# A hybrid attention layer on one core: the first output products placed among the last attention heads, operands in the tokens' tiles, and the end of mixer B left to the planner

## The chip, the core and the metric

The kernel runs on one core of one Trainium2 chip. The metric is device time in microseconds (us) for one execution. The core has a matrix engine (TensorE, "PE" in the profile, with its weight loads listed apart as "PEld"), three engines for elementwise work (VectorE "DVE", ScalarE "ACT", GpSimd "POOL") and a queue engine (SyncE "SP") that issues most of the DMA transfers. Each engine runs its own instructions in the order in which the program has them, and waits for the others by semaphores.

## The reference

One layer over 528 tokens (16 meta tokens and 512 real ones) of width 2048:

```python
hn = rmsnorm(h, pre_norm_g[layer])
proj = jnp.einsum('bld,dc->blc', hn, w_in[layer])
qa, ka, va, ga, qb, kb, vb, gb = jnp.split(proj, SPLIT_POINTS, axis=-1)
ya = gqa_axial_mixer(qa, ka, va, ...) * jax.nn.silu(ga)      # mixer A: 8 heads, 2 groups of keys
yb = diff_attn_mixer(qb, kb, vb, ...) * jax.nn.silu(gb)      # mixer B: 8 heads, differential, ALiBi
y = jnp.einsum('blc,cd->bld', jnp.concatenate([ya, yb], axis=-1), w_out[layer])
h = h + rmsnorm(y, post_norm_g[layer])
return h[:, N_META:, :]
```

Each mixer has heads of width 128. Only the 512 real tokens leave the layer.

## The kernel before

**Arithmetic.** Every large product is made from split operands: `x` is kept as a high part `xh` and a rest `xl`, a weight chunk as `wh` and `wl`, and a product is three matmuls (high by high, rest by high, high by rest). A weight chunk is 128 partitions by 1024 numbers (512 KB). SP loads it into `st`, ACT rounds it to `wh` (L156), DVE subtracts for `wl` (L157). `st`, `wh` and `wl` have three buffers each (pool `wp`, L115), and `fetch` (L199) keeps two chunks ahead of the one in use; the list `todo` sets their order.

**Stages.** First come the columns of mixer B, head by head: `dense_T` (L205) makes transposed columns by 16 steps `k` over the tokens' tiles `xh[k]`, `xl[k]`. Then mixer A's keys and values, the queries of both groups (`queries_A`, L678: four PSUM banks, 192 matmuls of 512 columns), the second group's keys and values, and eight gates (`dense_T(REAL)` in the loop at L841, 48 matmuls of 512 columns each). Last comes the output product.

**The planner.** The heads' work is written as generators (`attention_B`, `attention_A`, `p_times_v`, `finish_B`), and `Lanes` (L41) places it between the dense matmuls. It keeps a planned clock, which each matmul advances. `poll` (L81), called after each group of three dense matmuls, resumes a generator that is due; a generator says by `yield LAG[...]` how much later it is due again. `finish` (L96) and `finish_all` (L100) force: they resume generators one after the other until a head is done, with no dense matmul in between. PE keeps this order exactly. The planned clock is no measurement; it only sets the order. Transposes, `pv` and `ss` share two PSUM buffers (`tr`, pool `ptr`), so each of them also waits until ACT and DVE have read the one before the last.

**The two forced places.** After mixer A's first keys and values, L818 (`finish_head(NH - 1)`) forces the rest of mixer B's last head, since the queries of group 0 take over buffers of that head (`ql`) and the zeros `zed` (L819) take over those of `dist`. After the last gate, `gate_A(7, ...)` (L842, L555) and L845 force the rest of mixer A's last head. Then the attention's pools and the tokens' tiles are released (L846, L847), and the pools of the output product are opened in their place.

**The output product.** It is made as a Strassen-like scheme: 14 products of four weight chunks each (`product`, L936), a product being 48 matmuls of 512 columns into two PSUM banks (`po`). The columns of the output are taken in two pairs of blocks, `PAIRS` (L721). For a pair, `first_half` (L989) makes the product of operand `b0` (mixer B's heads, first half of the tokens), that of `t1` (difference of their halves), copies both to `y`, and adds the product of `of_a(0)` to the first bank pair and of `of_a(1)` to the second; `of_a` reads mixer A's gated heads `oh`/`ol`. Then come `t2`, `t3` and `t4`, sums of halves of both mixers. Some weight chunks are sums of blocks, made in DRAM beforehand (`ws`, `weigh`, L737). The gated heads reach these operands through DRAM (`oscr`): SP writes a head out (L543, L560) and reads it back in the layout that the product needs (L890, L901, L907), and ACT and DVE split it. `gpB` (1024 KB, the post-norm gains, L922) and the residual `xr` (L965) are loaded in this stage too. At the end of it rows are normalised and added to the residual (L1034 to L1081).

Of the kernel before, what the change touches and what calls it, by code (L numbers as in the profile page):

```python
# [17 lines left out]
P = 128  # L18
DM = 2048
# [86 lines left out]
def kernel(ctx: ExitStack, tc: tile.TileContext, xT, xn, xm, w_s, w_t, w_q, w_o,  # L106
# [571 lines left out]
    def queries_A(g):  # L678

        pss = [pd.tile([P, 512], F32, name="pd", tag="pd") for _ in range(TT)]  # L680
        for k0 in range(0, KT, 2):
# [64 lines left out]

    def wlast(i):
# [109 lines left out]
    b0, t1 = [[[op.tile([P, 2, NP], F32R, name=f"{n}{x}{i}", tag=f"{n}{x}{i}") for x in "hl"]
               for i in range(4)] for n in "ab"]
    oh, ol = [[op.tile([P, SEQ], F32R, name=f"o{x}{j}", tag=f"o{x}{j}") for j in range(NH)]
              for x in "hl"]  # L860
    t4 = [[op.tile([P, 2, NP], F32R, name=f"t4h{i}", tag=f"t4h{i}"),
           yp.tile([P, 2, NP], F32R, name=f"t4l{i}", tag=f"t4l{i}")] for i in range(4)]
    pad(op, "opad", 224)
    t3 = operand("t3", (yp, yp), 0, 1)
    yp.tile([P, 512], F32, name="jko", tag="jko")
    pad(yp, "ypad", 384)


    y = [[None] * 4 for _ in range(TT)]

    def fill(places):
        for t, g in places:
            y[t][g] = ytile(t, g)

    fill([(t, 3) for t in range(TT)])
    gpB = yp.tile([P, DM], F32, name="gpB")
    fill([(t, g) for t in range(3) for g in (1, 2)])
    fill([(t, 0) for t in range(TT)])
    pad(yp, "zpad", 128)
    t3 += operand("t3", (yp, yp), 1)  # L880
    t2 = operand("t2", (yp, yp))
    fill([(3, 1), (3, 2)])
    ssy = [yp.tile([P, 4], F32, name=f"ssy{t}", tag=f"ssy{t}") for t in range(TT)]
    sspart = [yp.tile([P, 1], F32, name=f"ssp{t}", tag=f"ssp{t}") for t in range(TT)]

    of_B = []
    for i in range(4):
        for g, half in ((3, lo_), (0, hi_)):
            st = y[i][g].rearrange("p (i q) -> p i q", i=2)
            nc.sync.dma_start(out=st, in_=oscr[i].rearrange("i p q -> p i q")[:, :, half])  # L890
            of_B.append(st)
    for i in range(4):
        st, sd = of_B[2 * i:2 * i + 2]
        split(b0[i], st)
        TTv(out=sd, in0=st, in1=sd, op=SUB)
        split(t1[i], sd)

    def bring_A(j):

        st = y[j // 2][1 + j % 2]  # L900
        nc.sync.dma_start(out=st, in_=oscr[4 + j // 2][j % 2])  # L901
        hi(oh[j], st)
        lo(ol[j], st, oh[j])

    def half_of(i, half):
        t = gp.tile([P, 2, NP], F32, name="ts", tag="g", bufs=4)
        load(t, oscr[i].rearrange("i p q -> p i q")[:, :, half])  # L907
        return t

    def sums_of_heads():  # L910
        for i in range(4):

            b1, r, c0, a0 = [half_of(n, half) for n, half in ((i, hi_), (4 + i, hi_), (i, lo_),
                                                              (4 + i, lo_))]
            for to, x, y_, op_ in ((t3, b1, r, SUB), (t2, r, c0, SUB), (t4, r, a0, ADD)):
                TTv(out=r, in0=x, in1=y_, op=op_)
                split(to[i], r)
                yield

    sum_steps = sums_of_heads()  # L920

    nc.sync.dma_start(out=gpB, in_=gpost)  # L922

    def square(t, g, src):
        jk = yp.tile([P, 512], F32, name="jko", tag="jko")
        at = (0, 1, 3, 2)[g]
        return nc.scalar.activation(jk, src, AF.Square, accum_out=ssy[t][:, at:at + 1])

    def by_gain(t, g, src=None):
        return TTv(out=y[t][g], in0=y[t][g] if src is None else src,  # L930
                   in1=gpB[:, g * 512:(g + 1) * 512], op=ALU.mult)
# [57 lines left out]
    def first_half(p, pool, tasks):  # L989


        r0, r1 = PAIRS[p]
        pa = product(of_t(b0), banks(pool), beside=tasks[0])
        rank[0] = 40
        for u, ps in enumerate(pa):
            nc.scalar.activation(y[u][r1], ps, AF.Copy)
        pb = product(of_t(t1), banks(pool), beside=tasks[1])
# [21 lines left out]
    for j in range(4):  # L1019
        bring_A(j)  # L1020
# [122 lines left out]
```

## Time and profile before

| | us |
|---|---|
| median of three runs (944.68 to 946.38) | 945.44 |
| the profiled execution | 945.67 |
| its span, first to last instruction | 943.9 |
| PE busy | 911.0 |
| DVE busy | 589.4 |
| ACT busy | 505.1 |
| POOL busy | 121.5 |

Matmuls overlap each other in PE's pipeline, so a row's duration is longer than the distance to the next row: a dense 512-column matmul has rows of 0.39 us that start 0.23 us apart. What a matmul costs is that distance. An idle stretch of PE stands in brackets behind the row that ends it, with the instruction that released it. "PEclk" is the clock that PE was granted as a share of full speed.

### The profile page before, as it was taken

The page shows a single profiled execution, that of the slowest core. Times are in us where ns is not written, and L with a number is a line of the kernel's source. Part 1 is how long each engine was busy: PE and PEld are TensorE (multiplying, and loading weights), DVE is VectorE, ACT ScalarE, POOL GpSimd, SP SyncE. Part 2 cuts the span into 40 slices and gives each one's busy share as a digit, 9 for nine tenths or more (in the row PEclk, how much of TensorE's full clock was granted, in tenths as well). Part 3 has the DMA queues.
Part 4 walks back from the last instruction along what each step waited for, and adds up shares of the span by engine and source line. Part 5 has one row for each costly group of instructions (what it writes and reads, how often), then busy time and mean ns, then how long its engine had stood idle before and what let it go on. Part 6 is the DMA issues. An engine that isn't in the chain of part 4 may idle for free.

```text
span 943.9 us, 14282 instructions
## 1 busy us (share of the span) xinstructions
PE 911.0 (97%) x5450; PEld 804.2 (85%) x5450; DVE 589.4 (62%) x1041; ACT 505.1 (54%) x877; POOL 121.5 (13%) x168
## 2 busy tenths in 40 slices
PE   9999999999999999999969999899999988999995
PEld 7999898989989899998958888888788876888884
DVE  6576675747575574856652464965454457766887
ACT  6564655647464563746632536556555546655552
POOL 0102120111112011110100201421111100000012
PEclk9999999999999999999979999999999999999998
DMA  9837645856848476682213322121212248879764
GB/s 327 288 112 222 158 136 136 235 130 181 210 118 241 122 199 170 172 219 68 80 45 101 89 91 68 45 67 57 79 57 90 79 135 307 280 257 329 262 214 178
DMA packets 52979, 149.86 MB, mean 159 GB/s; under 512 B 7920, under 2 KB 14960, under 8 KB 52528
## 3 DMA queue, kind: packets, MB, share of 16 engines
q1 hardware_dynamic: 48160, 132.18, 42.0%
q0 software_dynamic: 4608, 16.78, 10.3%
q8 instruction: 42, 0.69, 0.3%
q14 instruction: 25, 0.20, 0.1%
q10 hardware_dynamic: 144, 0.01, 0.0%
HBM read 140.55 MB, written 41.94 MB: 193 GB/s over the span
## 4 chain that ended last, share of the span: by engine, by line
PE 86%; DVE 5%; ACT 4%; DMA 3%; issue 1%; POOL 1%; SPq 0%; DVEq 0%; ACTq 0%; POOLq 0%
PE pd L60 57%; PE po L60 13%; PE sc L60 6%; PE pv L60 5%; PE tr L63 4%; DVE wl L157 1%; DVE y L1041 1%; DMA gpB<-in_gpost_dram 1%; ACT wh L156 1%; DMA st<-ws 1%; DMA xs<-in_xT_dram 1%; DMA st<-in_w_o_dram 0%; POOL ssh L245 0%; ACT jk L616 0%; PE ss L60 0%
## 5 line engine op out<-in xcount | busy, mean ns | idle before, releaser
L60 PE MATMUL pd<-xh,wh 128*128 128x264 f32 (+1 forms) x992 | 333.8, 337 | 0.2 <-ACT xh L184 0.2
L60 PE MATMUL pd<-xl,wh 128*128 128x264 f32 (+1 forms) x992 | 323.4, 326 | 0.4 <-DVE xl L185 0.4
L60 PE MATMUL pd<-xh,wl 128*128 128x264 f32 (+1 forms) x992 | 323.1, 326 | 0.1
L156 ACT ACTIVATE wh<-st 128x1024 fp32r<-128x1024 f32 (+2 forms) x159 | 165.7, 1042 | 231.1 <-PE pd L60 98.9
L157 DVE TENSOR_TENSOR wl<-st,wh 128x1024 fp32r<-128x1024 f32 (+2 forms) x159 | 191.3, 1203 | 118.5 <-ACT wh L156 117.3
L60 PEld LDWEIGHTS pd<-xh,wl 128*128 128x128 f32 x992 | 186.6, 188 | 16.3 <-DVE wl L157 0.3
L60 PEld LDWEIGHTS pd<-xh,wh 128*128 128x128 f32 x992 | 187.1, 189 | 11.7 <-ACT xh L184 0.7
L60 PEld LDWEIGHTS pd<-xl,wh 128*128 128x128 f32 x992 | 187.5, 189 | 10.1 <-DVE xl L185 0.8
L505 ACT ACTIVATE p<-p,mx 128x528 f32<-128x528 f32 x64 | 47.0, 734 | 43.2 <-DVE mx L497 43.0
L63 PE MATMUL tr<-ident,p 128*128 128x128 f32 (+1 forms) x320 | 50.9, 274 | 4.3 <-DVE qlA L333 3.2
L497 DVE CUSTOM_DVE_ANT_0 p<-sc,dist 128x528 f32<-128x528 f32 x64 | 44.8, 701 | 11.4 <-PE sc L60 11.0
L333 DVE TENSOR_TENSOR pl<-tr,ph 128x512 fp32r<-128x512 f32 x64 | 43.1, 686 | 13.1 <-ACT ph L330 12.4
L60 PE MATMUL pd<-wh,xh 128*128 128x512 f32 x128 | 51.2, 400 | 0.0
L60 PE MATMUL pd<-wh,xl 128*128 128x512 f32 x128 | 50.6, 396 | 0.0
L60 PE MATMUL pd<-wl,xh 128*128 128x512 f32 x128 | 50.5, 394 | 0.0
L330 ACT ACTIVATE ph<-tr 128x512 fp32r<-128x512 f32 x64 | 37.5, 592 | 23.5 <-PE tr L63 23.2
L63 PEld LDWEIGHTS tr<-ident,p 128*128 128x128 f32 (+1 forms) x320 | 37.1, 132 | 14.4 <-DVE qlA L333 3.8
L512 DVE SCALAR_TENSOR_TENSOR p<-p,c 128x528 f32<-128x528 f32 x32 | 24.5, 766 | 31.0 <-POOL p L510 31.0
L741 POOL DMA_DIRECT2D ws<-in_w_o_dram x32 | 26.7, 835 | 120.1 <-DMA ws<-in_w_o_dram 66.1
L599 POOL TENSOR_SCALAR p<-p,smA 128x528 f32<-128x528 f32 x32 | 23.4, 733 | 145.2 <-DVE smA L598 129.0
L510 POOL TENSOR_SCALAR p<-p,sm 128x528 f32<-128x528 f32 x32 | 23.5, 735 | 138.4 <-DVE sm L507 127.4
L457 POOL TENSOR_SCALAR pm<-pm 32x256 fp32r<-32x256 f32 x32 | 21.2, 662 | 143.7 <-ACT pm L330 140.9
(222 smaller groups left out, 1605.5 us busy)
## 6 DMA issues: line engine op xcount, KB each, us to landing
st<-in_w_t_dram SPq DMA_DIRECT2D x82, 512.0 KB, 4.2
ws<-in_w_o_dram POOLq DMA_DIRECT2D x32, 512.0 KB, 8.4
st<-ws SPq DMA_DIRECT2D x32, 512.0 KB, 4.9
st<-in_w_o_dram SPq DMA_DIRECT2D x24, 512.0 KB, 3.9
ws<-in_w_o_dram SPq DMA_DIRECT2D x16, 512.0 KB, 6.1
ws<-ws SPq DMA_DIRECT2D x16, 512.0 KB, 5.4
st<-in_w_q_dram SPq DMA_DIRECT2D x16, 512.0 KB, 3.5
xs<-in_xT_dram SPq DMA_DIRECT2D x16, 264.0 KB, 5.5
```

Of the source, the lines that this page charges most:

```text
L60: self._add(self.nc.tensor.matmul(out, lhsT, rhs, start=start, stop=stop, **kw), us)
L63: self._add(self.nc.tensor.transpose(out, in_, ident), 0.109)
L156: splits.append((nc.scalar.activation(wh[:, c], st[:, c], AF.Copy), nc.vector.tensor_tensor(out=wl[:, c], in0=st[:, c], in1=wh[:, c].bitca ...
L157: nc.vector.tensor_tensor(out=wl[:, c], in0=st[:, c], in1=wh[:, c].bitcast(F32), op=ALU.subtract)))
L330: nc.scalar.activation(dst, src, AF.Copy)
L333: nc.vector.tensor_tensor(out=dst, in0=src, in1=h.bitcast(F32), op=ALU.subtract)
L497: nc.vector.tensor_tensor_reduce(out=two(p), in0=sc[:, :, :HALF], in1=two(dist[:, w0:w0 + NT]), scale=-0.125 / slope(h), scalar=3.0e38, op ...
L505: nc.scalar.activation(p2[m], p2[m], AF.Exp, scale=-1.0, bias=mx[:, m:m + 1], accum_out=sm[:, m:m + 1])
L510: nc.gpsimd.tensor_scalar(out=p2[0], in0=p2[0], scalar1=sm[:, 0:1], scalar2=1.0, op0=ALU.mult, op1=ALU.mult)
L512: nc.vector.scalar_tensor_tensor(out=p2[0], in0=p2[1], scalar=c2, in1=p2[0], op0=ALU.mult, op1=ALU.add)
L599: nc.gpsimd.tensor_scalar(out=p, in0=p, scalar1=sm, scalar2=1.0, op0=ALU.mult, op1=ALU.mult)
L741: nc.gpsimd.dma_start(out=dst, in_=src, accum_op=ALU.add)
```

## The change

No instruction is added or taken away on any engine: PE has 5450, DVE 1043, ACT 718, POOL 173 and SP 320 rows in the program's order both before and now. What changes is where they stand and which buffers they use.

- **Tokens' tiles.** Each `xh[k]`, `xl[k]` is now a tag of its own (`xtile`) in a pool that lives to the end, and an operand of the output product takes over one such buffer at a time (`otile`): `b0` and `t1` those of k 0 to 7, `oh`/`ol` those of k 8 to 15, later `t4`, `xr` and the last weights. Before, all were released at once.
- **First products.** `come` brings mixer B's heads back from DRAM during gate 5; `half_dead`, called in the last gate after its step k = 8, splits them into `b0` and `t1`. The products `b0` and `t1` of pair 0 stand ahead of `lanes.finish_all()`, and `product` now polls. Those of pair 1 follow at once (`held`), and only then the parts with `of_a`.
- **Gates.** `gate_A` is cut in two; a head's gating is finished one gate later, and the last after the first two products.
- **Heads' steps.** `scA` goes from 4.6 to 5.4.
- **Mixer B's end.** `finish_head(NH - 1)` and the zeros are called by `queries_A(0, zeros)` after its matmuls, ahead of the reads of its banks.
- **Loads.** The residual's second half is loaded during `t3`, no longer during `t2`, and into the buffers of `t2`.

```diff
-... qA=2.35, scA=4.6, pA=4.14, ...
+... qA=2.35, scA=5.4, pA=4.14, ...
...
+    def xtile(name, n, dt=F32R):
+        return xp.tile([P, 576], dt, name=name, tag=f"x{n}")
+    xh, xl = [[xtile(f"x{n}{k}", 2 * k + j)[:, :NT] for k in range(KT)]
+              for j, n in enumerate("hl")]
...
-    def gate_A(h, pss):
-        finish_head(NH + h)
+    def silu_A(pss):
         g = gp.tile([P, SEQ], F32, name="gt", tag="gt")
         nc.vector.tensor_tensor(out=g, in0=pss[0], in1=rB[:, NM:], op=ALU.mult)
         nc.scalar.activation(g, g, AF.Silu)
+        return g
+
+    def gate_A(h, g):
         nc.vector.tensor_tensor(out=oA[h], in0=oA[h], in1=g, op=ALU.mult)
...
-    def queries_A(g):
+    def queries_A(g, before=None):
...
+        if before:
+            before()
         res = []
...
     for p in range(2):
         todo += [block(p, 0, 0, i) for i in range(4)] + sums[p][0]
+    for p in range(2):
         todo += [block(p, 0, 1, i) for i in range(4)] + sums[p][2]
...
-    finish_head(NH - 1)
-    zed.append(ap.tile([P, DW], F16, name="zed", tag="dist", bufs=1))
-    nc.vector.memset(zed[0], 0.0)
-    start_heads(0, *queries_A(0), kA, vA)
+    def zeros():
+        finish_head(NH - 1)
+        zed.append(ap.tile([P, DW], F16, name="zed", tag="dist", bufs=1))
+        nc.vector.memset(zed[0], 0.0)
+
+    start_heads(0, *queries_A(0, zeros), kA, vA)
...
+    def come(n, i, half):
...
+        nc.sync.dma_start(out=t, in_=oscr[i].rearrange("i p q -> p i q")[:, :, half])
+        return t
...
+    def half_dead():
+        for to, n in ((b0, 0), (t1, 8)):
+            for i in range(4):
+                st, sd = of_B[2 * i:2 * i + 2]
+                to.append([two_(otile(f"{'ab'[n // 8]}{x}{i}", n + 2 * i + j))
+                           for j, x in enumerate("hl")])
+                if n:
+                    TTv(out=sd, in0=st, in1=sd, op=SUB)
+                    st = sd
+                split(to[i], st)
+
     for h in range(NH):
-        gate_A(h, dense_T(REAL))
-    lanes.finish_all()
-    att.close()
-    xst.close()
+        if h == 5:
+            of_B += [come(2 * i + j, i, half) for i in range(4)
+                     for j, half in enumerate((lo_, hi_))]
+        gates.append(dense_T(REAL, half=half_dead if h == NH - 1 else None))
+        if h:
+            finish_head(NH + h - 1)
+            gate_A(h - 1, silu_A(gates[h - 1]))
+    gate_7 = silu_A(gates[NH - 1])
...
+    held = [[product(of_t(b0), banks(pd))]]
+    rank[0] = 40
+    held[0].append(product(of_t(t1), banks(pd)))
+    lanes.finish_all()
+    gate_A(NH - 1, gate_7)
+    att.close()
...
+    evict(0)
+    nc.sync.dma_start(out=gpB, in_=gpost)
+    for j in range(2):
+        bring_A(j)
...
+    held.append([product(of_t(b0), banks(pd2), beside=lambda i: i < 3 and [
+        bring_A(j) for j in (2 + 2 * i, 3 + 2 * i)])])
+    held[1].append(product(of_t(t1), banks(pd2), beside=lambda i: next(sum_steps)))
+    evict(1)
+    first_half(0, (two_by, two_by))
     nc.scalar.activation(warm, ssy[1][:, 0:1], AF.Sqrt)
-    held.append(first_half(1, pd, (two_by, two_by, sum_and_load, sum_and_load)))
-    second(0, pd2, held[0], lambda i: residual())
-    second(1, pd, held[1], lambda i: residual())
+    first_half(1, (sum_and_load, sum_and_load))
+    second(0, pd, held[0][1], None)
+    second(1, pd2, held[1][1], None)
...
-    third = [product(of_t(t3), banks(pd2))]
+    third = [product(of_t(t3), banks(pd), beside=lambda i: residual())]
```

How this moves instructions is shown at three places. **PE, the end of mixer B.** Before, the last matmul of mixer A's first values (`pd<-xh,wl`) is followed by the rest of mixer B's last head: transposes of its probabilities `p`, of mixer A's `vf`, `kn` and `km`, then the products `pv`:

```order
L60 MATMUL pd<-xh_144,wh 128x264
L60 MATMUL pd<-xl_145,wh 128x264
L60 MATMUL pd<-xh_144,wl 128x264
L63 MATMUL tr<-ident,p 128x128 x8
L63 MATMUL tr<-ident,vf 128x128 x4
L63 MATMUL tr<-ident,p 32x128 x2
L63 MATMUL tr<-ident,kn 128x128 x4
L63 MATMUL tr<-ident,vf 16x128
L63 MATMUL tr<-ident,km 128x16
L60 MATMUL pv<-ph,vh 128x256
```

Now (from the second transpose group on) dense matmuls of the queries, `pd<-wh,xh`, stand between them:

```order
L63 MATMUL tr<-ident,p 128x128 x4
L60 MATMUL pd<-wh,xh_115 128x512
L60 MATMUL pd<-wh,xl_131 128x512
L60 MATMUL pd<-wl,xh_115 128x512
L60 MATMUL pd<-wh,xh_115 128x512
L60 MATMUL pd<-wh,xl_131 128x512
L60 MATMUL pd<-wl,xh_115 128x512
L63 MATMUL tr<-ident,p 128x128 x4
L60 MATMUL pd<-wh,xh_114 128x512
L60 MATMUL pd<-wh,xl_130 128x512
L60 MATMUL pd<-wl,xh_114 128x512
L63 MATMUL tr<-ident,vf 128x128 x4
```

All of that stretch (16 large transposes, four small ones, 13 `pv` and two `ss` matmuls) now lies in the first half of the queries' 192 matmuls. **PE, the end of mixer A.** Before, the last `pv` matmuls of its last head stand in one run ahead of the first output product, `po<-wh,ah` (`ah`, `al` are the parts of `b0`):

```order
L60 MATMUL pv<-ph,vh 128x256
L60 MATMUL pv<-ph,vl 128x256
L60 MATMUL pv<-pl,vh 128x256
L60 MATMUL pv<-pm,vm 128x256
L60 MATMUL po<-wh,ah_7965 128x512
L60 MATMUL po<-wh,al_7966 128x512
L60 MATMUL po<-wl,ah_7965 128x512
L60 MATMUL po<-wh,ah_7965 128x512
```

Now the same `pv` matmuls stand inside the second chunk of that product:

```order
L60 MATMUL po<-wh,ah_7887 128x512
L60 MATMUL po<-wh,al_7888 128x512
L60 MATMUL po<-wl,ah_7887 128x512
L60 MATMUL pv<-ph,vh 128x256
L60 MATMUL pv<-ph,vl 128x256
L60 MATMUL pv<-pl,vh 128x256
L60 MATMUL pv<-ph,vh 128x256
L60 MATMUL pv<-ph,vl 128x256
L60 MATMUL pv<-pl,vh 128x256
L60 MATMUL po<-wh,ah_7887 128x512
L60 MATMUL po<-wh,al_7888 128x512
L60 MATMUL po<-wl,ah_7887 128x512
```

The rest of that head is over within the first product's 48 matmuls, and nothing is left for `finish_all`. **SP, around the gains' load.** Before, `gpB` stands behind the loads of mixer B's heads, and with the loads of mixer A's heads (`y<-oscr`) ahead of the second chunk of summed weights (`st<-ws`):

```order
L890 DMA y_8024<-oscr_84 128x2x256
L922 DMA gpB<-in_gpost_dram 128x2048
L901 DMA y_8015<-oscr_85 128x512
L901 DMA y_8016<-oscr_85 128x512
L901 DMA y_8017<-oscr_86 128x512
L901 DMA y_8018<-oscr_86 128x512
L901 DMA y_8019<-oscr_87 128x512
L901 DMA y_8020<-oscr_87 128x512
L901 DMA y_8040<-oscr_88 128x512
L149 DMA st<-ws_561 128x1024
L901 DMA y_8041<-oscr_88 128x512
L149 DMA st<-ws_562 128x1024
```

Now the loads of mixer B's heads are far ahead of this place, and a weight chunk stands between each one or two of the others; the one write `oscr<-oA` is the last head's:

```order
L148 DMA st<-ws_562 128x1024
L978 DMA gpB<-in_gpost_dram 128x2048
L148 DMA st<-ws_563 128x1024
L566 DMA oscr_88<-oA_7925 128x512
L148 DMA st<-in_w_o_dram 128x1024
L954 DMA y_8177<-oscr_85 128x512
L148 DMA st<-in_w_o_dram 128x1024
L954 DMA y_8178<-oscr_85 128x512
L148 DMA st<-in_w_o_dram 128x1024
L954 DMA y_8181<-oscr_86 128x512
L954 DMA y_8182<-oscr_86 128x512
L148 DMA st<-in_w_o_dram 128x1024
```

More of the change, by code (lines that the diff above doesn't have):

```diff
@@ L857 @@
[L857 to L931, printed above, removed]
+    def come(n, i, half):
+        tag = "ql" if n < 4 else "f" if n < 6 else "tT"
+        t = ap.tile([P, NT if tag == "tT" else SEQ], F32, name="ob", tag=tag,
+                    bufs=2 if tag == "tT" else 4)[:, :SEQ]
+        t = t.rearrange("p (i q) -> p i q", i=2)
+        nc.sync.dma_start(out=t, in_=oscr[i].rearrange("i p q -> p i q")[:, :, half])
+        return t
@@ new lines, in two_ @@
+    def two_(t):
+        return t.rearrange("p (i q) -> p i q", i=2)
+    b0, t1, of_B, gates = [], [], [], []
+    def half_dead():
[8 more added lines that the diff above has]
+                split(to[i], st)
@@ new lines @@
+    for h in range(NH):
+        if h == 5:
[6 more added lines that the diff above has]
+    gate_7 = silu_A(gates[NH - 1])
+    rank[0] = 0
+    oh, ol = [[otile(f"o{x}{j}", 16 + 2 * j + n) for j in range(NH)] for n, x in enumerate("hl")]
@@ new lines, with evict, bring_A @@
+    gpB = yp.tile([P, DM], F32, name="gpB")
+    pad(yp, "ypad", 256)
+    t2, t3 = [operand(n, (yp, yp)) for n in ("t2", "t3")]
+    t4 = []
+    ssy = [yp.tile([P, 4], F32, name=f"ssy{t}", tag=f"ssy{t}") for t in range(TT)]
+    sspart = [yp.tile([P, 1], F32, name=f"ssp{t}", tag=f"ssp{t}") for t in range(TT)]
+    def evict(p):
+        for pss, t in zip(held[p], (0, 2)):
+            for u, ps in enumerate(pss):
+                nc.scalar.activation(y[t + u][PAIRS[p][1]], ps, AF.Copy)
+    def bring_A(j):
+        st = y[j // 2][j % 2]
+        nc.sync.dma_start(out=st, in_=oscr[4 + j // 2][j % 2])
+        hi(oh[j], st)
+        lo(ol[j], st, oh[j])
@@ new lines, in half_of, with sums_of_heads @@
+    def half_of(i, half):
+        t = gp.tile([P, 2, NP], F32, name="ts", tag="g", bufs=4)
+        load(t, oscr[i].rearrange("i p q -> p i q")[:, :, half])
+        return t
+    def sums_of_heads():
+        for i in range(4):
+            t4.append([two_(otile(f"t4{x}{i}", 8 + 2 * i + j)) for j, x in enumerate("hl")])
+            b1, r, c0, a0 = [half_of(n, half) for n, half in ((i, hi_), (4 + i, hi_), (i, lo_),
+                                                              (4 + i, lo_))]
+            for to, x, y_, op_ in ((t3, b1, r, SUB), (t2, r, c0, SUB), (t4, r, a0, ADD)):
+                TTv(out=r, in0=x, in1=y_, op=op_)
+                split(to[i], r)
+                yield
@@ new lines, with square, by_gain @@
+    sum_steps = sums_of_heads()
+    evict(0)
+    nc.sync.dma_start(out=gpB, in_=gpost)
+    for j in range(2):
+        bring_A(j)
+    def square(t, g, src):
+        jk = yp.tile([P, 512], F32, name="jko", tag="jko")
+        at = (0, 1, 3, 2)[g]
+        return nc.scalar.activation(jk, src, AF.Square, accum_out=ssy[t][:, at:at + 1])
+    def by_gain(t, g, src=None):
+        return TTv(out=y[t][g], in0=y[t][g] if src is None else src,
+                   in1=gpB[:, g * 512:(g + 1) * 512], op=ALU.mult)
@@ L987, in part, with first_half @@
                                 op1=ALU.add)
[L989 to L997, printed above, removed]
-        for u, ps in enumerate(pb):
-            nc.scalar.activation(y[2 + u][r1], ps, AF.Copy)
-        product(of_a(0), pa, more=True, beside=tasks[2])
+    def first_half(p, tasks):
+        r0 = PAIRS[p][0]
+        pa, pb = held[p]
+        product(of_a(0), pa, more=True, beside=tasks[0])
         for u, ps in enumerate(pa):
@@ L1003, in first_half @@
             by_gain(u, r0, ps)
-        return product(of_a(1), pb, more=True, beside=tasks[3])
+        product(of_a(1), pb, more=True, beside=tasks[1])
     def second(p, pool, pb, beside):
@@ L1017, in every @@
         return lambda i: do() if i % n == n - 1 else None
-    for j in range(4):
-        bring_A(j)
-    two_by = every(2, lambda: next(sum_steps, None))
-    held = [first_half(0, pd2, (lambda i: bring_A(4 + i), None, two_by, two_by))]
-    nc.scalar.activation(warm, ssy[1][:, 0:1], AF.Sqrt)
     def sum_and_load(i):
@@ L1060 @@
     ry = {}
-    third = [product(of_t(t3), banks(pd2))]
+    third = [product(of_t(t3), banks(pd), beside=lambda i: residual())]
     for u, ps in enumerate(third[0]):
         third_done(2 + u, ps)
-    third.append(product(of_t(t3), banks(pd)))
+    third.append(product(of_t(t3), banks(pd2), beside=lambda i: residual()))
     for u, ps in enumerate(third[1]):
```

32 lines of the change are left out of this document (18 added, 14 removed).

## The prediction

> **What bounds the kernel now.** I read the page first: its busy line, its slices and its chain by engine.
>
> ```profile
> span 943.9 us, 14282 instructions
> PE 911.0 (97%) x5450; PEld 804.2 (85%) x5450; DVE 589.4 (62%) x1041; ACT 505.1 (54%) x877; POOL 121.5 (13%) x168
> ...
> PE   9999999999999999999969999899999988999995
> ...
> DMA  9837645856848476682213322121212248879764
> ...
> PE 86%; DVE 5%; ACT 4%; DMA 3%; issue 1%; POOL 1%; SPq 0%; DVEq 0%; ACTq 0%; POOLq 0%
> ```
>
> PE is the bound: it carries 86% of the chain, and nearly every slice is full. As the change adds no instruction to any engine, it can only win or lose time in which PE waits or runs at a lowered clock. So I looked for that time, with PE's timeline, in three places: the dent in slice 21 (from 472 us), the thin slices of mixer A's heads (550 to 770), and the dent in slices 33 and 34, where the output products begin. The start and the tail are left as they are.
>
> **Place 1, the end of mixer B.** PE's timeline, start and duration first, the idle time before a row in brackets; then one stretch of the windows, with PE, PEld, DVE, ACT and POOL busy and the granted clock behind them:
>
> ```profile
> 474.07 1.04 PE L63 MATMUL tr<-ident,p 128*128 128x128 f32 x8
> 478.16 0.65 PE L63 MATMUL tr<-ident,vf 128*128 128x128 f32 x4 [3.05 <-DVE pl L333]
> ...
> 480.23 1.12 PE L63 MATMUL tr<-ident,kn 128*128 128x128 f32 x4 [1.08 <-DVE vl L333]
> ...
> 482.76 0.29 PE L63 MATMUL tr<-ident,km 16*128 16x16 f32 x1 [1.20 <-DVE kl L333]
> ...
> 488.00 0.50 PE L60 MATMUL ss<-sh,ones_r 128*128 128x512 f32 x1 [1.79 <-ACT sh L330]
> ...
> 489.07 0.39 PE L60 MATMUL pd<-wh,xh 128*128 128x512 f32 x1
> ...
> 492.70 0.63 PE L60 MATMUL pd<-wh,xl 128*128 128x512 f32 x1
> ...
> 493.41 0.39 PE L60 MATMUL pd<-wh,xh 128*128 128x512 f32 x1
> 493.63 0.39 PE L60 MATMUL pd<-wh,xl 128*128 128x512 f32 x1
> ...
> 484.00:486.00 2.00, 2.00 (x11) 1.91 (x9) 0.00 (x0) 0.00 (x0) 0.00 (x0) 0.50 0.00 0
> ```
>
> The forced head takes from 474.07 to 489.07, 15.0 us, mostly waits on ACT and DVE for small pieces, and its `pv` matmuls run at a clock of 0.50. What the same instructions cost at full speed stands at the end of mixer A, in the chain and in PE's timeline:
>
> ```profile
> 764.33 0.44 PE tr L63 x4
> ...
> 767.99 0.22 PE tr L63 x2
> ...
> 770.13 0.28 PE L60 MATMUL pv<-ph,vh 128*128 128x256 f32 x1
> ...
> 771.54 0.28 PE L60 MATMUL pv<-pm,vm 96*128 96x256 f32 x1
> ```
>
> Sixteen transposes at 0.44 per four make 1.8 us, four small ones at 0.22 per two 0.4, 13 `pv` at (771.54 - 770.13) / 12 = 0.118 make 1.5, two `ss` at 0.23 make 0.5: 4.2 us. So 15.0 - 4.2 = 10.8 us are lost. Behind them, 12 matmuls from 489.07 to 493.41 take 4.34 us where 12 x 0.228 = 2.7 is the full rate: 1.6 more. **Place 1 loses 12.4 us.**
>
> **Place 2, the first output products.** PE's timeline again, then two steps of the chain in time:
>
> ```profile
> 772.82 0.50 PE L60 MATMUL po<-wh,ah 128*128 128x512 f32 x1 [0.99 <-ACT ah L330]
> ...
> 777.28 0.51 PE L60 MATMUL po<-wh,ah 128*128 128x512 f32 x1 [0.77 <-ACT ah L330]
> ...
> 792.02 0.50 PE L60 MATMUL po<-wh,bh 128*128 128x512 f32 x1 [2.80 <-ACT wh L156]
> ...
> 797.27 0.40 PE L60 MATMUL po<-wh,bh 128*128 128x512 f32 x1
> ...
> 933.06 0.39 PE L60 MATMUL po<-wl,t4h 128*128 128x512 f32 x1
> ...
> 776.74 7.68 DMA gpB<-in_gpost_dram
> 784.43 6.46 DMA st<-ws
> ```
>
> From 797.27 to the last matmul at 933.06 the remaining 599 steps take 0.2267 us each, without a gap. The first 72 of the 672 matmuls take 24.45 us (772.82 to 797.27) where 72 x 0.2267 = 16.3 would do: 8.1 lost, to operands that came late at first, then to a weight chunk that landed behind `gpB` and the heads' loads. With the 1.2 us from the end of the last `pv` (771.54 + 0.12) to 772.82, **place 2 loses 9.3 us.**
>
> **Place 3, mixer A's heads.** All longer waits of PE between 493 and 769 but one (0.73 at 622), two stretches of the windows, and ACT's rows ahead of one wait:
>
> ```profile
> 599.14 1.12 PE L63 MATMUL tr<-ident,p 128*128 128x128 f32 x4 [2.63 <-DVE qlA L333]
> ...
> 625.27 0.28 PE L63 MATMUL tr<-ident,kfA 128*16 128x128 f32 x1 [0.74 <-ACT oA L604]
> ...
> 673.79 0.39 PE L60 MATMUL sc<-kh,qh 128*128 128x264 f32 x1 [1.09 <-ACT qh L330]
> ...
> 696.22 0.66 PE L63 MATMUL tr<-ident,p 128*128 128x128 f32 x4 [0.55 <-DVE qlA L333]
> ...
> 711.13 0.39 PE L63 MATMUL tr<-ident,p 128*32 128x128 f32 x2 [1.17 <-DVE pl L333]
> ...
> 590.00:600.00 10.00, 7.37 (x60) 7.16 (x58) 9.13 (x26) 6.84 (x25) 8.14 (x9) 0.95 0.16 53
> 600.00:610.00 10.00, 10.00 (x76) 9.97 (x75) 9.15 (x25) 3.11 (x7) 2.21 (x4) 0.88 0.18 54
> ...
> 671.13 1.28 ACT L597 ACT_TABLE_LOAD   x1
> 672.43 0.73 ACT L597 ACTIVATE p<-p,mxA 128x528 f32<-128x528 f32 x1
> ...
> 673.16 0.57 ACT L330 ACTIVATE qh<-tr 128x512 fp32r<-128x512 f32 x1
> ```
>
> The five waits and the one at 622 sum to 6.9 us, and ten microseconds at a clock of 0.88 lose 1.2: **place 3 loses 8.1 us.**
>
> **The change part by part.** The sum starts from the profiled execution, 945.67 us, which is 1.8 above its span and 0.2 above the median of the three runs; I let the 1.8 stand.
>
> *Mixer B's end.* The order shows three to six dense matmuls (0.7 to 1.4 us) between any two pieces of the head. They cover the chain of ACT and DVE that frees a transpose's buffer, and the whole head fits in the queries' 192 x 0.228 = 43.8 us. PE no longer idles long enough to meet the 0.50 clock. The added wait is that of the queries' third bank on DVE's `vf`; the first two banks have 12 matmuls, 2.7 us, to run ahead of it. Without the cover the rows' waits (3.05 + 1.08 + 1.20 + 1.79 = 7.1) would come back. I take the full **-12.4**, bounds -12.4 and -5.3.
>
> *First products among the last heads.* The eight loads of mixer B's heads move to gate 5, where the DMA line shows 1 or 2 tenths, so they cost nothing. The splits into `b0` and `t1` take ACT and DVE some 5 and 8 us (8 and 12 steps of the sizes below) in the last gate's second half, where 21 matmuls, 13 `pv` and eight transposes (about 7 us) lie between k = 8 and the first product. Each `b0` part is needed one chunk (12 x 0.227 = 2.7 us) after the one before, and two such steps take less.
>
> ```profile
> L330 ACT ACTIVATE ah<-y 128x512 fp32r<-128x512 f32 x4 | 2.5, 625 | 2.3 <-DMA y<-oscr 2.3
> L333 DVE TENSOR_TENSOR al<-y,ah 128x512 fp32r<-128x512 f32 x4 | 2.7, 686 | 1.6 <-ACT ah L330 1.6
> ```
>
> The last head is over inside the first product; its gating, its way through DRAM and the splits of `oh`/`ol` have the other three early products, 3 x 10.9 = 33 us, before `of_a` is needed. So the whole **-9.3** goes, bounds -9.3 and -4.4 (should the crowded loads repeat the 2.80 with its 0.53 and 1.6 of slow clock, 4.9).
>
> *What is late next: the loads of the held products.* Over the 38 us (14 chunks of 2.72) from `gpB`'s issue, SP now asks for 14 chunks (7.3 MB), `gpB` (1.05), eight heads (2.1), two rounds of `ts` (2.1) and one write (0.3): 12.9 MB, 338 GB/s. The trace has moved more, share and GB/s being the last two columns:
>
> ```profile
> 784.00:788.00 4.00, 4.00 (x20) 3.30 (x19) 2.63 (x5) 2.51 (x5) 0.00 (x0) 1.00 1.05 403
> 850.00:860.00 10.00, 10.00 (x46) 8.29 (x45) 6.58 (x8) 5.00 (x9) 0.00 (x0) 1.00 0.98 340
> ```
>
> At 340 the demand just fits, and 850 to 860 held it with PE full; at 403 it has room. [...] I take **+1** for a late chunk, bounds 0 and +9.8 (two crowded places at 4.9).
>
> *Heads' steps and gates.* Each head's planned steps are 2.4 us longer, so waits of a step on the one before get shorter. But the causes in place 3 stay: around 596 DVE is full (9.13 of 10) with the second queries' norms, and at 673 the copy `qh` stands behind a table load and an Exp that a gate's Silu brought; the heads' queries still come due by the same `qA`. The rows do not show the new spacing, so the bounds are -8.1 (all gone) and +8.1 (as much again). I take half, **-4**, nearer to the rows that go than to the ones that could come. The residual's move to `t3` and the order of the weight chunks cost nothing: that stage had DMA room and PE never waited there.
>
> Sum: 945.67 - 12.4 - 9.3 + 1 - 4 = **921.0 us**.
>
> **The rivals.** *A, everything is regained:* no new wait and place 3 clean: 945.67 - 12.4 - 9.3 - 8.1 = 915.9. For it: identical work and PE the only bound. Against: DVE's full stretch. *B, the small pieces still wait among the queries:* their transposes share two buffers, and the waits of 7.1 come back: 921.0 + 7.1 = 928.1. Against it: the dense matmuls between them. *C, the held products are crowded:* gaps of the kind at 792 at two places: 921.0 - 1 + 9.8 = 929.8. For it: 338 GB/s over 38 us; against it: one or two loads between chunks instead of fifteen in a row. *D, slower:* weights of the held products come one at a time. If each of the eight chunks of pair 1 lands as late as that behind `gpB` (6.46 us, where PE uses one in 2.72), it costs 8 x 3.74 = 29.9: 920.0 + 29.9 = 949.9. It decides once landing takes longer than the two chunks of lead, 5.4 us, in every round. *E, the change does not take effect,* as the order found new forced stretches: 945. The order shows none.
>
> **How the numbers follow.** Forecast 0.55 (917.5 to 925), A 0.15, B 0.12, C 0.14, D 0.03, E 0.01. The range 915.5 to 928.5 holds the forecast, A and B, and leaves out C, D and E, 0.18. A measurement tells 0.2% (1.9 us) from no change; faster by more than that is everything but D and E: 0.96; same 0.01; slower 0.03.
>
> **What would show it.** Right: PE's timeline has no wait over 1 us in the queries of group 0 and no granted clock under 1.00 there; the first `po` matmul follows the last gate matmul or transpose without a wait; the 672 `po` matmuls take little over 672 x 0.227 + 2 us for the head inside them; PE busy falls below 900, as the 0.50 stretch goes. Place 3 is wrong if its waits sum to under 2 or over 6 us. A wait on `wh` or `wl` behind `gpB` or `ts` in pair 1 would be C, waits on `tr` at the queries B. The prediction is wrong if the heads wait more than before with their wider steps.

## The result, and the profile after

The changed kernel takes 922.04 us (median of four runs, 921.88 to 922.33) where the kernel before, run beside it, took 945.06: ratio 0.9759, 95% interval 0.974 to 0.9777. Forecast were 921.0 us and a range of 915.5 to 928.5. The profiled execution took 921.97 us with a span of 920.2.

The head of its page: busy time, the slices of PE, and the chain by engine.

```profile
span 920.2 us, 14275 instructions
PE 901.2 (98%) x5450; PEld 798.7 (87%) x5450; DVE 588.4 (64%) x1041; ACT 503.4 (55%) x877; POOL 122.0 (13%) x168
...
PE   9999999999999999999999999998999999999995
...
PE 87%; DVE 7%; ACT 2%; DMA 2%; issue 1%; POOL 0%; SPq 0%; DVEq 0%; ACTq 0%; POOLq 0%
```

The dents of slices 21, 33 and 34 are gone. PE's busy time fell by 9.8 us (911.0 to 901.2) at the same 5450 matmuls. Some 7.5 us of that are matmuls that ran at a clock of 0.50 before and no longer do (half of PE's busy time in the five falls of the clock before the tail; the last section tells of them); the other 2.3 us are not broken down here. The rest of the gain is waiting. By stages, each ended by the start of its last matmul in PE's timeline:

| us | before | after | difference |
|---|---|---|---|
| to the end of mixer A's first values | 473.95 | 472.97 | -0.98 |
| from there to the end of group 0's queries (place 1) | 60.05 | 48.33 | -11.72 |
| from there to the end of the gates (place 3) | 235.90 | 233.50 | -2.40 |
| from there to the last output product (place 2) | 163.16 | 154.62 | -8.54 |
| tail, to the end of the span | 10.84 | 10.78 | -0.06 |

**Place 1 after.** PE's timeline of the changed kernel (the only wait over 0.2 us there, and the last matmul of the queries), and one stretch of its windows:

```profile
473.09 0.40 PE L60 MATMUL pd<-wh,xh 128*128 128x512 f32 x1
...
483.19 0.23 PE L63 MATMUL tr<-ident,km 16*128 16x16 f32 x1 [0.23 <-DVE pm L337]
...
521.30 0.39 PE L60 MATMUL pd<-wl,xh 128*128 128x512 f32 x1
...
484.00:486.00 2.00, 2.00 (x13) 1.72 (x11) 0.00 (x0) 0.00 (x0) 0.00 (x0) 1.00 0.60 229
```

The same two microseconds of the span stood at a clock of 0.50 before. **Place 2 after.** PE's timeline: the first output matmul, the last head's pieces inside the product, the last matmul; then two stretches in which the held products run.

```profile
754.80 0.40 PE L60 MATMUL pd<-xh,wl 128*128 128x512 f32 x1
755.04 0.60 PE L63 MATMUL tr<-ident,p 128*128 128x128 f32 x4
755.39 0.48 PE L60 MATMUL po<-wh,ah 128*128 128x512 f32 x1
...
756.86 0.38 PE L63 MATMUL tr<-ident,p 128*32 128x128 f32 x2
...
909.42 0.39 PE L60 MATMUL po<-wl,t4h 128*128 128x512 f32 x1
...
770.00:780.00 10.00, 10.00 (x46) 8.27 (x45) 5.55 (x6) 4.45 (x6) 0.00 (x0) 1.00 0.97 344
780.00:790.00 10.00, 10.00 (x46) 8.29 (x45) 8.51 (x10) 8.72 (x14) 0.00 (x0) 1.00 0.75 265
```

No wait over 0.2 us stands between 755 and 909; the loads reach 344 GB/s beside a full PE. **Place 3 after.** Four of its waits in PE's timeline, the two longest among them, and the stretch that had a clock of 0.88:

```profile
587.48 0.39 PE L63 MATMUL tr<-ident,p 128*32 128x128 f32 x2 [1.79 <-DVE pl L337]
...
601.16 0.66 PE L63 MATMUL tr<-ident,kfA 128*128 128x128 f32 x4 [0.78 <-DVE pl L337]
...
606.17 0.66 PE L63 MATMUL tr<-ident,p 128*128 128x128 f32 x4 [0.51 <-ACT oA L610]
...
624.36 0.66 PE L63 MATMUL tr<-ident,vf 128*128 128x128 f32 x4 [1.85 <-DVE kl L337]
...
600.00:610.00 10.00, 8.70 (x72) 8.25 (x70) 5.14 (x16) 6.41 (x21) 3.44 (x6) 1.00 0.26 80
```

All waits over 0.2 us here sum to 6.7 us, against 7.1 before (the 6.9 of the prediction and 0.2 at 674). They are nearly as long in sum, but other waits; the longest is 1.85 instead of 2.63, and the clock stays at 1.00.

**The loads of mixer B's heads.** They do not run in gate 5, as the text of the change and the prediction have it. Gate 5's first matmul starts at 705.99; SP's timeline has the first and the last of the eight loads long before, around the start of gate 0 (618.57):

```profile
600.91 0.43 SPq L862 DMA_DIRECT2D ob<-oscr  x1
...
629.46 0.36 SPq L862 DMA_DIRECT2D ob<-oscr  x1
```

### The profile page after: what moved, and what is told of

It reads as the page before. It is cut to its first block, busy times and chain, and to the rows that moved or that the text cites. A ratio compares the mean times of both kernels' runs of the same rounds, so it can differ in the third digit from the quotient of the medians.

```text
span 920.2 us, 14275 instructions
## 1 busy us (share of the span) xinstructions
PE 901.2 (98%) x5450; PEld 798.7 (87%) x5450; DVE 588.4 (64%) x1041; ACT 503.4 (55%) x877; POOL 122.0 (13%) x168
## 4 chain that ended last, share of the span: by engine, by line
PE 87%; DVE 7%; ACT 2%; DMA 2%; issue 1%; POOL 0%; SPq 0%; DVEq 0%; ACTq 0%; POOLq 0%
PE pd L60 58%; PE po L60 14%; PE sc L60 6%; PE pv L60 5%; PE tr L63 4%; DVE wl L156 1%; DVE y L1064 1%; DMA st<-in_w_s_dram 1%; DVE p L600 1%; DMA ob<-oscr 1%; DMA st<-in_w_o_dram 0%; DVE pl L337 0%; ACT p L603 0%; PE ss L60 0%; DVE y L988 0%
## 5 line engine op out<-in xcount | busy, mean ns | idle before, releaser
L603 ACT ACTIVATE p<-p,mxA 128x528 f32<-128x528 f32 x32 | 23.5, 735 | 41.4 <-DVE mxA L600 41.4
```

The costliest lines, as they stand in the source:

```text
L603: nc.scalar.activation(p, p, AF.Exp, scale=-1.0, bias=mx, accum_out=sm)
```

## The experiments

The kernel before was run again beside each group of runs. Its medians were 945.06 us beside the changed kernel, 947.47 beside e1 to e4, 945.98 beside e5, e6, e7 and e10, and 945.40 beside c_after, e9, e11 and e12. Where less than two microseconds decide, the stages of the traces are compared. The stages, as in the table above:

| us | start | place 1 | place 3 | place 2 | median of runs |
|---|---|---|---|---|---|
| e1_open_B | 473.04 | 48.34 | 234.93 | 162.69 | 932.29 |
| e2_steps_46 | 473.55 | 48.33 | 238.11 | 153.88 | 925.34 |
| e3_late_loads | 473.06 | 48.34 | 231.48 | 155.17 | 920.99 |
| e4_force_A | 473.64 | 48.34 | 235.22 | 156.95 | 926.50 |
| e5_more_dma | 472.76 | 48.34 | 233.08 | 155.04 | 924.59 |
| e6_norms_8 | 472.80 | 48.33 | 231.46 | 155.02 | 920.62 |
| e7_warm_B | 473.13 | 59.06 | 235.85 | 162.86 | 943.86 |
| e9_loads_last | 473.57 | 48.32 | 231.44 | 165.06 | 931.67 |
| e10_late_norms | 472.96 | 48.34 | 231.57 | 154.74 | 921.11 |
| e11_later_norms | 473.21 | 48.34 | 230.23 | 155.35 | 919.12 |
| e12_steps_60 | 473.63 | 48.34 | 231.25 | 154.69 | 920.94 |
| c_after | 473.31 | 48.32 | 233.07 | 154.62 | 921.78 |

**e1_open_B: mixer B's end alone.** In the kernel before:

```diff
-    finish_head(NH - 1)
-    zed.append(...)
-    nc.vector.memset(zed[0], 0.0)
-    start_heads(0, *queries_A(0), kA, vA)
+    start_heads(0, *queries_A(0, zeros), kA, vA)
```

> The kernel before with one edit: mixer B's last head is no longer forced ahead of group 0's queries. Theory of the sum (the parts add, and place 1 loses about 12 us by itself): 945.1 - 11.7 to 12.4 = 932.5 to 934; no wait of PE over 1 us between 470 and 500, granted clock 1.00 there, the other two places as before. Rival 1 (given back later: mixer A's heads, shifted against the queries, wait more): 936 to 941, with PE waits between 570 and 760 summing to over 10 us. Rival 2 (the gain belongs to the change as a whole): 943 or more.

Measured 932.29 us (932.03 to 933.55), ratio 0.9855 (0.9827 to 0.9883). Place 1 falls from 60.05 to 48.34 us, as far as in the whole change, and place 2 stays as it was. Place 3 is 1.0 us shorter, though its waits over 0.2 us sum to 7.5 us against 7.1: no fall of the clock follows its wait of 2.62 us. The parts add; both rivals fall.

**e2_steps_46 and e12_steps_60: the width of the heads' steps.** In the changed kernel:

```diff
-... qA=2.35, scA=5.4, ...
+... qA=2.35, scA=4.6, ...
```

That is e2; in e12 the number is 6.0.

> The changed kernel with the step scA back from 5.4 to 4.6. Theory W (the 2.4 us that place 3 gained come from the wider steps): 924 to 926, and PE's waits between 570 and 760 sum to 8 us or more, against 6.7 in the changed kernel. Rival S (place 3 gained because the slow clock of 600 to 610 went and the heads stand elsewhere; the step size is of no account): 921 to 923.

> The changed kernel with the step scA at 6.0 instead of 5.4 (4.6 gave 925.3). Theory W (wider steps shorten the waits, and there is more to be had): 920 to 921.5, waits of PE between 570 and 760 below 5 us. Rival S (5.4 is wide enough, the rest are waits that the step does not reach): 921.6 to 922.8. Rival T (at some width the steps of two heads meet): 923 or more.

Measured 925.34 us (924.39 to 926.60) at 4.6 and 920.94 (919.66 to 922.01) at 6.0, against 921.78 at 5.4 in c_after, beside e12. PE's waits over 0.2 us in place 3 sum to 8.1, 6.7 and 4.3 us from the narrow step to the wide. So theory W holds: the width counts. Of the step to 6.0 the waits tell more than the median, whose 0.8 us lie within the scatter of the executions. At 4.6 the wait of 2.63 us of the kernel before is back, and in the trace a lowered clock from 586 to 593 costs 3.4 us, more than the 1.4 us of waits that were added. That is the profiled execution, the longest of the four (926.60, mean granted clock 0.992); two others have a clock of 0.997 and still take 924.39 and 926.08 us.

**e3_late_loads and e9_loads_last: when the loads of mixer B's heads stand.** In e3 the loads, and the splits of `half_dead` with them, are kept behind the last gate; the loads are held in program order (`tc.keep_in_program_order`, not shown):

```diff
-        if h == 5:
-            of_B += [come(2 * i + j, i, half) for i in range(4) ...]
-        gates.append(dense_T(REAL, half=half_dead if h == NH - 1 else None))
+        gates.append(dense_T(REAL))
...
     gate_7 = silu_A(gates[NH - 1])
+    of_B += [come(2 * i + j, i, half) for i in range(4) ...]
+    half_dead()
```

In e9, which has e3's edit too, two more lines put the forced end, the gating and the writing of the last head ahead of them:

```diff
     gate_7 = silu_A(gates[NH - 1])
+    finish_head(2 * NH - 1)
+    gate_A(NH - 1, gate_7)
     of_B += [come(2 * i + j, i, half) for i in range(4) ...]
...
     lanes.finish_all()
-    gate_A(NH - 1, gate_7)
```

> The changed kernel with one edit: the eight loads of mixer B's heads stay behind the last gate instead of rising to gate 5. Theory O (late operands are the larger part of place 2): the first product waits for ah and al as before and meets a lowered clock, 927 to 931. Rival K (the weight chunk behind the gains and the loads was the larger part): 922 to 924.5.

> The changed kernel with mixer A's last head forced to its end, gated and written out ahead of the loads of mixer B's heads, and these loads ahead of the first output product: place 2 in the kernel before's order, but in the new buffers. Theory O (operands that come late are the larger part of place 2): 2.3 us for the forced end, some 8 us until the first operands are loaded and split, and a lowered clock, 930 to 936. Rival K (mostly the weight chunk behind the gains): 925 to 928.

e3 measured 920.99 us (920.62 to 922.10): both of its expectations were wrong, since the loads were still issued at 742 us and landed in time, and place 3 got shorter by 1.6 (against c_after) to 2.0 us (against the changed kernel's first trace). What had been costly there is seen in DVE's timeline of the changed kernel:

```profile
620.59 0.69 DVE L877 TENSOR_TENSOR ob<-ob 128x512 f32<-128x512 f32 x1 [2.12 <-DMA ob<-oscr]
621.20 0.70 DVE L600 CUSTOM_DVE_ANT_0 p<-sc,zed 128x528 f32<-128x528 f32 x1
...
623.03 0.67 DVE L877 TENSOR_TENSOR ob<-ob 128x512 f32<-128x512 f32 x1
623.62 0.68 DVE L337 TENSOR_TENSOR kl<-tr,kh 128x512 fp32r<-128x512 f32 x1
```

The first subtraction for `t1` had been ordered up to the loads and held DVE for 2.12 us until its operand landed; a head's score (L600), a second subtraction and `kl` stood behind it, and PE waited for `kl` until 624.36. In e3 that wait is gone: windows of e3, the stretch that has 8.15 us of PE in the changed kernel.

```profile
620.00:630.00 10.00, 9.71 (x55) 7.58 (x54) 5.58 (x12) 5.87 (x14) 1.76 (x3) 1.00 0.15 54
```

e9, whose operands do come late, measured 931.67 us (930.01 to 934.01), ratio 0.9851 (0.982 to 0.988): 10.7 above e3. PE's timeline and windows of e9:

```profile
756.50 0.38 PE L60 MATMUL pv<-ph,vh 128*128 128x256 f32 x1 [2.12 <-DVE pl L337]
...
764.09 0.80 PE L60 MATMUL po<-wh,ah 128*128 128x512 f32 x1 [5.63 <-ACT ah L334]
...
760.00:770.00 10.00, 5.91 (x17) 4.47 (x18) 4.88 (x8) 3.83 (x7) 0.00 (x0) 0.59 0.75 237
```

With the forced end, the loads behind it, and the clock that falls in the meantime, place 2 is back at 165.06 us (163.16 before), within theory O's numbers. But e9 is not the kernel before's order, as its expectation has it. SP's timeline of the kernel before, then of e9:

```profile
766.08 0.90 SPq L890 DMA_DIRECT2D y<-oscr  x2
773.09 0.33 SPq L560 DMA_DIRECT2D oscr<-oA  x1
773.52 3.12 SPq L890 DMA_DIRECT2D y<-oscr  x6
...
759.63 0.32 SPq L566 DMA_DIRECT2D oscr<-oA  x1
760.00 4.05 SPq L862 DMA_DIRECT2D ob<-oscr  x8
```

In the kernel before two of the eight loads stand ahead of the last head's write; in e9 all stand behind it, and no weight chunk comes late. So e9 shows what late operands cost when they come last. What they cost in the kernel before is read from its own rows: PE's waits for `ah` and `al` sum to 2.4 us (0.99 + 0.40 + 0.77 + 0.22), while the weight chunk behind the gains costs 2.80 + 0.53 of waits and 1.7 of lowered clock, 5.0 us. There rival K was the larger part. No run puts that chunk alone back.

**e4_force_A: only the end of the last head forced**, its operands early:

```diff
+    finish_head(2 * NH - 1)
     held = [[product(of_t(b0), banks(pd))]]
```

> The changed kernel with one edit: mixer A's last head is forced to its end ahead of the first output product, its operands still there early. Theory F (a forced end costs the chain of ACT and DVE behind each transposed piece, as at place 1): two or three waits of 1 to 2 us before the first product, 925 to 928. Rival N (a head with as little left as this one costs nothing; in the kernel before only 0.99 us stood behind its forced end): 922 to 923.

Measured 926.50 us (924.71 to 927.06). One wait of 2.12 us stands before the `pv` matmuls, where theory F had two or three, and place 2 is 2.33 us longer than in the changed kernel. So F's mechanism holds at a price below its own: 922.0 + 2.3 = 924.3 us lies between the two forecasts. Another 1.7 us of the profiled execution (927.04) are a lowered clock in place 3, behind a wait of 2.02 us at 625, which the changed kernel has too (1.85, where the clock stayed). What lengthened the other executions is not known. In the kernel before, the forced end had no wait: its 13 `pv` matmuls take 1.5 us behind the last gate matmul, and its transposes stand ahead of that.

**e5_more_dma: more traffic beside the held products.**

```diff
     nc.sync.dma_start(out=gpB, in_=gpost)
+    for i in range(3):
+        spare = dr.tile([P, 1024], F32, ...)
+        tc.keep_in_program_order(nc.sync.dma_start(out=spare, in_=block(0, 0, 0, i)))
```

> The changed kernel with three more copies of 512 KB from DRAM to DRAM, issued behind the gains' load; nothing reads them. Theory R (the held products' loads have room): over the 38 us behind the gains 12.9 + 1.6 = 14.5 MB are asked for, 381 GB/s, under the 403 that the trace has shown; 921.5 to 923, no wait of PE over 0.5 us on wh or wl. Theory C (340 GB/s is about all that the queue carries here, rival C of the prediction): 14.5 / 0.340 = 42.6 us for 38, a wait of PE on weights and a lowered clock, 925 to 929.

In the profiled execution theory R holds. Windows of e5:

```profile
770.00:780.00 10.00, 10.00 (x46) 8.28 (x45) 4.36 (x4) 5.13 (x7) 0.00 (x0) 1.00 0.99 370
780.00:790.00 10.00, 10.00 (x45) 8.27 (x45) 8.06 (x11) 7.65 (x12) 0.00 (x0) 1.00 1.00 379
```

PE is full while 379 GB/s pass, at a DMA share of 1.00, and no wait for `wh` or `wl` is left. But the four executions lie at 922.64, 922.66, 926.52 and 926.68 us, the profiled one among the lower; c_after, without the copies, has one at 926.52 among three at 921.6 to 921.84. So the loads of the change itself had room to spare; whether the copies lengthen some executions isn't settled.

**e7_warm_B: how much of place 1 is clock.** In the kernel before, the end still forced:

```diff
+    cold = pd.tile([P, 512], F32, name="cold", tag="pd")
+    for task in (heads[NH - 1], over[NH - 1]):
+        task = task or over[NH - 1]
+        while not task[3]:
+            lanes.force()
+            for _ in range(2):
+                tc.keep_in_program_order(nc.tensor.matmul(cold, xh[0][:, :P], xh[0][:, NM:], ...))
```

> The kernel before, mixer B's end forced as it was, with two matmuls of 512 columns (their result is not read) behind each resumed piece, 22 in all, 5.0 us at full clock. Theory W (of the 12.4 us at place 1 some 5 are the lowered clock that the idle time brings, the rest waits): the clock stays at 1.00, the forced stretch takes 11.3 to 13 us instead of 15.0 and nothing is lost behind it, so from the end of mixer A's values to the first matmul of group 1's queries 54.9 to 56.6 us instead of 60.2, and 940 to 942 in all. Rival (the matmuls only push the pieces back, or the clock falls all the same): 59 us or more there, 944 to 947 in all.

Measured 943.86 us (941.52 to 945.47), ratio 0.9978 (0.9965 to 0.9991); place 1 takes 59.06 us. Theory W failed. PE's timeline and windows of e7:

```profile
477.32 0.66 PE L63 MATMUL tr<-ident,vf 128*128 128x128 f32 x4 [2.11 <-DVE pl L333]
...
478.00:480.00 2.00, 2.00 (x8) 1.34 (x8) 1.11 (x2) 0.97 (x2) 0.40 (x1) 0.55 0.59 225
480.00:482.00 2.00, 2.00 (x9) 1.38 (x7) 0.64 (x1) 0.82 (x2) 0.00 (x0) 0.60 0.00 0
482.00:484.00 2.00, 2.00 (x12) 1.70 (x12) 0.51 (x3) 0.49 (x3) 0.00 (x0) 1.00 0.00 0
```

The first wait only shrank from 3.05 to 2.11 us, and the clock fell behind it all the same; two of the three falls of the kernel before at this place went. Two such matmuls behind each piece did not keep the clock up here, and they won 1.0 us of the 11.7 that the dense matmuls of the queries win.

**e6_norms_8, e10_late_norms, e11_later_norms: what is left in place 3.** The second queries' norms are spread on the planned clock; e10 and e11 also have e3's edit:

```diff
-                yield LAG["norm"]
+                yield LAG["norm"] if g == 0 else 8.0
```

In e11 they also begin later:

```diff
-        return res, lanes.spawn(turn(), 0.0)
+        return res, lanes.spawn(turn(), 0.0 if g == 0 else 12.0)
```

> The changed kernel with the norms of the second group's queries set 8.0 apart on the planned clock instead of 4.0. Theory D (PE's waits from 587 to 611, 3.8 us in sum, come from these norms, which fill DVE there): they fall below 1.5 us in sum, 919 to 920.5. Rival M (the norms, moved, meet the second keys' norms at 610 to 630 and the waits turn up there): 921.5 to 924.

> The changed kernel with both edits: the loads of mixer B's heads kept behind the last gate (as in e3_late_loads, 921.0) and the second queries' norms 8.0 apart (as in e6_norms_8). If the two waits are separate (DVE's full stretch at 587, the subtractions at 620), they add: 918 to 919.5. If the norms only move the waits: 920.5 to 922.

> The changed kernel with the loads of mixer B's heads behind the last gate, and the second queries' norms begun 12 later on the planned clock and 8.0 apart. PE's order is that of e3_late_loads; on DVE only four rows of the norms stand between the two scores where there were thirteen. Theory D2 (PE's wait of 2 us at 587 is the head's score standing behind the norms on DVE): that wait falls below 0.7, 919 to 920.3. Rival (the wait comes from ACT or from the transposes' two buffers): it stays, 920.6 to 921.6.

e6 measured 920.62 us (920.14 to 923.14), e10 921.11 (920.00 to 921.51), e11 919.12 (918.70 to 919.79), ratio 0.9716 (0.9686 to 0.9745). In e6 the waits at 601 and 606 went, but the one at 587 stayed (2.06 us), so theory D was half right; e10 brought nothing over e3, against the expectation that the two add, and in its trace the clock fell behind a wait of 2.01 us. Why the wait at 587 stays, DVE's and ACT's timelines of the changed kernel tell:

```profile
579.62 1.50 DVE L625 SCALAR_TENSOR_TENSOR qn<-qn,ssh,gqB 128x128 f32<-128x128 f32 x4
582.11 0.35 DVE L625 SCALAR_TENSOR_TENSOR qn<-qn,ssh,gqB 128x128 f32<-128x128 f32 x1 [1.00 <-POOL ssh L249]
...
583.99 0.68 DVE L640 TENSOR_TENSOR qn<-qn,t 128x512 f32<-128x512 f32 x1
584.59 0.70 DVE L600 CUSTOM_DVE_ANT_0 p<-sc,zed 128x528 f32<-128x528 f32 x1
...
585.39 0.73 ACT L603 ACTIVATE p<-p,mxA 128x528 f32<-128x528 f32 x1 [3.44 <-DVE mxA L600]
...
586.12 0.57 ACT L334 ACTIVATE ph<-tr 128x512 fp32r<-128x512 f32 x1
...
586.74 0.69 DVE L337 TENSOR_TENSOR pl<-tr,ph 128x512 fp32r<-128x512 f32 x1
```

The norms of the second of the four tiles and the beginning of the third's stand ahead of a head's score on DVE. The third's first row (582.11) waits for POOL, ACT's Exp waits for the score, and the copy `ph` stands behind Exp; PE, 587.48, needs the buffer that `pl` frees last. Spacing alone (e6, e10) moves only the fourth tile, to 610 and 611. In e11 the third goes with it, behind 608. There the score runs at 581.53 and the wait at 587 is gone, as theory D2 has it, and place 3 is 2.8 us shorter than in c_after (1.3 shorter than in e3, whose edit it has too). **e11_later_norms is faster than both kernels**; it lies 2.7 us below c_after.

**c_after: the changed kernel again.**

> The changed kernel again, unaltered, beside the three that follow. It should come out at 921.5 to 922.6 as it did; if it lies above 923, differences of one us between runs of different calls are not to be read.

Measured 921.78 us (921.60 to 926.52), as expected; one execution of the four lies 4.7 higher.

## Why the prediction was right, step by step

- **Mixer B's end, -12.4:** -11.72 in the traces, by itself in e1. The queries and the head among them take 48.33 us, where 43.8 and 4.2 were reckoned. No small piece waited over 0.23 us (rival B).
- **First output products, -9.3 and +1:** -8.54. The late chunk (rival C, and D behind it) did not come: nothing waits between 755 and 909. The -9.3 was 0.8 too large, of which 0.5 are six transposes of the last head that now stand behind the last gate matmul, in place 2 instead of place 3; that the two errors leave only 0.2 is luck. Of the 8.5 us, the kernel before's rows put 5.0 on the weight chunk behind the gains, its clock included, and 2.4 on operands that came late, as the prediction read them; no run separates the two. e4 and e9 show what a forced end (2.33 us) and late operands would cost in the new order.
- **Heads' steps, -4:** -2.40. The mechanism named, shorter waits by wider steps, gave little in sum: 7.1 to 6.7 us of waits, over the 6 at which the prediction calls this place wrong. What went is the lowered clock: 1.7 us; no wait is over 1.85 us any more (the working had 1.2 for it, reading one stretch of two). The wider steps themselves take 1.4 us of waits (e2 against the changed kernel); the next point tells of a wait that came in. That "the causes in place 3 stay" was right for the norms on DVE, as e11 shows.
- **"The eight loads ... cost nothing" is the step that failed:** they found DMA room, but they ran some 75 to 105 us ahead of gate 5, the subtraction behind them was ordered up with them, and DVE waited 2.12 us for a landing, heads' work behind it. e3 shows 1.6 to 2.0 us in place 3, of which 0.5 comes back in place 2. Without this step place 3 would have come out as forecast: in e3 it takes 231.48 us, 4.4 less than in the kernel before (the clock's 1.7 among them), with waits of 4.9 us in sum.
- **The start, taken as unchanged, gave -0.98.** It is no part of the change: the stage's end lies between 472.76 and 473.95 us over all fourteen traces, and e1, with the start of the kernel before, has 473.04.
- **The sum:** 945.67 - 0.98 - 11.72 - 2.40 - 8.54 - 0.06 = 921.97, against 921.0. The terms missed by +0.7 (place 1), +1.6 (place 3), -0.2 (place 2 with its +1) and -1.0 (the start). That the sum is within 1 us owes something to the start, which the forecast had not in it; each place by itself came within 1.6 us.
- **The other signs:** no granted clock under 1.00 in the queries, and the first `po` matmul follows a transpose without a wait, as named. PE busy was to fall below 900; it fell to 901.2.

## What to carry to other kernels

A stretch in which a dependent chain is forced to its end cost twice here (place 1 of the kernel before), by its waits of over a microsecond (7.1 us in sum) and by the 10.2 us at a clock of 0.50 among and behind them; put it among dense matmuls that have to run anyway (place 1 got 11.7 us shorter by that), and read its full-rate cost from a place where the same instructions already run so. When a load is moved up because the DMA has room, look at what the scheduler moves up with it: here the subtraction that waited 2.12 us for a landing held a head's score and `kl`, which stood behind it on DVE, and PE waited 1.85 us. A remaining wait is found by going from PE's row back through ACT's and DVE's order until an instruction turns up that had no need to be there yet.

## What the hardware showed that was not expected

Ahead of the tail, the clock fell in pieces of one size. Read in strips of half a microsecond, a single fall is 3.4 us at a granted clock of 0.50, which by that clock is 1.7 us lost where PE is busy all through it (in the kernel before, the 12 matmuls around the one at 490 took 1.6 us more than at the full rate); longer ones are two or three such pieces (6.8 us at 479 in the kernel before, 10.2 at 758 in e9). The kernel before has a single one at the end of the wait at 599, in its windows:

```profile
596.00:598.00 2.00, 0.51 (x5) 0.29 (x3) 2.00 (x6) 0.16 (x2) 1.84 (x3) 1.00 0.00 0
598.00:600.00 2.00, 0.86 (x5) 0.86 (x5) 2.00 (x7) 1.95 (x4) 0.73 (x2) 0.76 0.00 0
600.00:602.00 2.00, 2.00 (x11) 2.00 (x10) 2.00 (x5) 0.60 (x1) 0.50 (x1) 0.50 0.00 0
602.00:604.00 2.00, 2.00 (x17) 2.00 (x16) 1.66 (x5) 0.78 (x2) 0.00 (x0) 0.89 0.28 53
```

e1 has the same wait (2.62 us, released by the same `qlA`) without a fall:

```profile
584.00:586.00 2.00, 0.00 (x0) 0.00 (x0) 2.00 (x7) 0.73 (x2) 1.34 (x2) 1.00 0.00 0
586.00:588.00 2.00, 1.50 (x13) 1.50 (x14) 2.00 (x6) 1.80 (x5) 1.17 (x1) 1.00 0.00 0
588.00:590.00 2.00, 2.00 (x20) 2.00 (x18) 2.00 (x5) 0.60 (x1) 0.00 (x0) 1.00 0.00 0
```

Over all fourteen traces, of nine waits of PE from 1.76 to 1.85 us one was followed by a fall (at 488.00 in the kernel before, with another 0.23 right behind it); of twelve from 2.01 to 2.63 us nine were; and of the three of 2.80 us or more two were, while behind the third (5.63 us in e9) a fall that had begun before it went on. So in these traces a fall followed some waits of 2.01 to 2.63 us and not others; what decides it no run here tells. If a part of it is chance, that would fit that executions of the kernel before spread over 942.68 to 948.78 us, and the four of e11, whose longest wait is 1.78 us, over 918.70 to 919.79. It is not shown: c_after and e5 have longest waits of 1.76 and 1.80 us in their traces, and yet three of their eight executions are some 4 us longer, at a mean granted clock of 0.993 or 0.994 where their others have 0.996 or 0.997. What the longer executions lost was not traced.
